# Laying each activation block of a seven-product block multiplication at an offset of its own within 64 bytes

## The chip, the cores and the metric

The kernel runs on one core of one Trainium2 chip. The metric is the time on the device in microseconds (us); the median of three runs stands for a kernel. Of every kernel there is also one profiled execution, whose span and instructions the tables below give.

## What is computed

One layer of a decoder over 528 positions (16 learned meta tokens and 512 tokens) of width 2048, all in float32: an input projection, eight heads of stick-breaking attention beside a gated short convolution, an output projection with residual, and a SwiGLU feed-forward part with residual. Only the feed-forward part, and the arrays that it works on, is touched here:

```python
n2 = _rmsnorm(h, g_ffn[l])                                     # 528 x 2048
h = h + (jax.nn.silu(n2 @ w_gate[l]) * (n2 @ w_up[l])) @ w_down[l]   # w_gate, w_up 2048 x 5632; w_down 5632 x 2048
return h[:, N_META:]
```

## The kernel before

Everything is transposed: channels lie on the 128 partitions, tokens along the free axis. To keep float32 accuracy with TensorE's faster fp32r operands, each operand is cut into a rounded part and a rest (`shi`, `slo` for weights; parts 0 and 1 of an activation block), and a product is three matmuls: rounded by rounded, rounded weight by rest, rest by rounded. Each takes 128x128 weights, and every MATMUL comes with an LDWEIGHTS of its own.

The feed-forward part takes a two by two block product with seven multiplications (Strassen's, in Winograd's form) in place of eight. The weights of a *pair* (gate and up rows of one of 44 groups of 128 hidden channels, or two groups of output channels) are four quadrants, and ACT and DVE form sums of them (`add_quads`, L564 and L584) and cut them in two (`split_quad`, L557 and L558). The activations are cut into four blocks (two halves of the tokens, two halves of the channels), from which seven activation blocks are made once, each `[128, 2, 8, 256]`: two parts, eight channel groups, 256 tokens. They stay in SBUF for the whole stage. These are the tiles `f0` to `f6` (`f_tile`, `fpool` and `fpool_last`). Two of the 44 groups are done beforehand as plain fp32 products; the other 42 go through `pair_product`, which calls `block_product` seven times, with blocks 0 to 6 in order. A `block_product` is, for each of eight channel groups k, the three matmuls of L609 to L611 with 256 moving columns from the activation block: 24 matmuls.

`gate` forms silu(gate) times up, the blocks of the next product, and `store_acts` cuts them and writes them to DRAM (`fd`, L772, on POOL's queue). The down projection walks over four chunks of the hidden dimension (6, 6, 5 and 5 groups deep); `load_acts` reads the seven blocks of a chunk back into a ring of twelve tiles `r0` to `r11` (L825, two DMAs a block, on POOL's queue), the first seven slots (`ring_a`) over the memory of `f0` to `f5`, the last five (`ring_b`) behind them, from the end of `f5` on. Each chunk has eight `pair_product`s whose `block_product`s are six or five groups deep: 18 or 15 matmuls. The ring also gives one tile, `hh`, for the residual in the last chunk.

The number of matmuls of L609 to L611 follows: 42 x 7 x 24 = 7056 on `f` tiles and 8 x 7 x 3 x (6 + 6 + 5 + 5) = 3696 on `r` tiles, 10752 in all, each with 256 columns.

The places of the tiles: a partition of SBUF is one row of bytes. Before, every `f` and `r` tile starts at a multiple of 64 bytes, and all tiles in one place mod 256; the weight tiles `shi` and `slo` start 32 bytes past a multiple of 64. Within a tile the step from group to group is 1024 bytes for activations and 512 for weights. The tile framework tracks every tile by its bytes: a tile that is laid where another one was waits for that one's last reader. In the stage before, operands stand otherwise: the weights `whi`, `wlo` of the projections at multiples of 64; the `nh`, `nl` tiles (normalised input) 32 past a multiple of 64, of which the products `pk` and `pv` take columns in two halves of 264 (the first at 32 past, the second at a multiple of 64), the convolution's products `pc` and `pu` two halves of 258 (at 16 and at 24 past), and `pq` and `pb` 512 columns at 32 past; the output projection `po` takes 512 columns at a multiple of 64 from `oah`, `oal`, `och`, `ocl`.

The order of instructions on each engine is that of the program; the split of the weights runs three block products ahead (`S_AHEAD`).

Of the kernel before, what the change touches and what calls it, by code (L numbers as in the profile page):

```python
# [15 lines left out]
P = 128  # L16
# [9 lines left out]
T2 = SEQ // 2  # L26
# [7 lines left out]
def hybrid_layer(ctx: ExitStack, tc: tile.TileContext, xT, w_in, w_out, w_gu, w_down, vecs, out):  # L34
# [12 lines left out]
    def open_pool(name, bufs=1, **kw):  # L47
        return tc.alloc_tile_pool(name=name, bufs=bufs, reuse_waits="tile", **kw)
# [166 lines left out]
    ms, r, eps_r2, r2 = accs[1], rpool.tile([P, L], F32, name="r"), accs[1], acc  # L215
# [486 lines left out]
    r_h = [acc_h[:, None, t * T2 : (t + 1) * T2].to_broadcast([P, 4, T2]) for t in range(2)]  # L702
    n_f = [0]

    def f_tile(dt, i):

        n_f[0] += 1
        pool = fpool if i < 6 else fpool_last
        return pool.tile([P, 2, 8, T2], dt, tag=f"f{i}", name=f"f{i}_{n_f[0]}")


    (a11, a21), (a12, a22) = ((b[:, 0], b[:, 1]) for b in blocks)
    acts = [None] * 7
    acts[:4] = [f_tile(F32R, i) for i in range(4)]
    w, v, u = (f_tile(F32, i) for i in (4, 5, 6))

    def halves_of_k(op, *blks):
# [12 lines left out]
    def split_act(i, src):  # L730
        if acts[i] is None:
            acts[i] = f_tile(F32R, i)
        halves_of_k(lambda h, l, s: split(h, l, s), acts[i][:, 0], acts[i][:, 1], src)
# [77 lines left out]
    rings_p = [open_pool("ring_a")]  # L811
    rings, n_ring = {}, [0]

    def ring_tile(dt, name):
        i = n_ring[0] % 12
        n_ring[0] += 1
        return rings_p[i // 7].tile([P, 2, 6, T2], dt, tag=f"r{i}", name=name)

    def load_acts(c, s):
        if c < len(CHUNKS):  # L820
            n = CHUNKS[c]
            rings[c, s] = ring_tile(F32R, f"r{c}_{s}")[:, :, :n]

            for part in range(2):
                gp.dma_start(rings[c, s][:, part], fd[c][s][:, part], max_dma_last_dim=3072)  # L825
# [6 lines left out]
    for c in range(len(CHUNKS)):  # L832
        end = c == len(CHUNKS) - 1
        if end:
            hh = ring_tile(F32, "hh")
        for j in range(KT // 2):

            if 1 <= j <= 5:
                load_acts(c + 1, j - 1)
            c1 = cpool.tile([P, 2, T2], F32, tag="c1", name=f"d1_{c}_{j}")  # L840
            c2 = cpool.tile([P, 2, T2], F32, tag="c2", name=f"d2_{c}_{j}")
            if end:
                h2 = [hh[:, :, 2 * (j % 3) + m] for m in range(2)]
                for m in (1, 0):
                    gp.dma_start(h2[m], two(hs[2 * j + m]))
            x = pair_product([rings[c, s] for s in range(7)], c1, c2)
            if j == KT // 2 - 1:
                for s in (5, 6):
                    load_acts(c + 1, s)
            if end:  # L850
                ve.tensor_tensor(c2, c2, h2[1], ALU.add)
                nc.sync.dma_start(two(out[2 * j + 1]), c2)
                ve.tensor_tensor(c1[:, 0], c1[:, 0], h2[0][:, 0], ALU.add)
                ve.tensor_tensor(c1[:, 1], x, h2[0][:, 1], ALU.add)
                nc.sync.dma_start(two(out[2 * j]), c1)
            else:
                sc.copy(c1[:, 1], x)
                gp.dma_start(two(hs[2 * j + 1]), c2, accum_op=ALU.add)
                gp.dma_start(two(hs[2 * j]), c1, accum_op=ALU.add)
# [59 lines left out]
```

## Time and profile before

| | |
|---|---|
| median of 3 runs | 2166.58 us (2165.41 to 2168.12) |
| profiled execution | 2165.52 us, span 2163.8 us |
| granted TensorE clock, mean | 0.995 |
| TensorE matmuls busy | 2136.8 us (99%) |
| weight loads busy | 2026.1 us (94%) |
| VectorE busy | 1551.9 us (72%) |
| ScalarE busy | 997.6 us (46%) |
| GpSimd busy | 378.7 us (18%) |
| mean DMA rate | 149 GB/s |

The span is the stretch from first to last instruction; the time of the execution has 1.7 us more. In the profile, PE is the matmuls and PEld the weight loads; a matmul's listed duration contains its passage through the array, so that successive matmuls overlap, and what one of them costs in a row of many is the distance from its start to the next one's start, called its pitch here. Idle time is put down to the instruction or DMA whose end came last.

### The profile page before, as it was taken

How to read it: one execution, taken by the hardware profiler on the slowest of the kernel's cores; microseconds unless marked ns; L12 is line 12 of the kernel's file. 1: busy time of each engine (PE TensorE's matmuls, PEld its weight loads, DVE VectorE, ACT ScalarE, POOL GpSimd, SP SyncE). 2: the span in 40 equal slices, each digit the busy share in tenths (PEclk: the TensorE clock that was granted, in tenths of full speed). 3: DMA queues.
4: the chain of work that ended last, by engine and by line, in shares of the span. 5: the costliest groups of instructions: out<-in, count | busy, mean ns of one | idle time of the engine just before them, and what ended most of it. 6: DMA issues, size and time to landing. Idle time of an engine off the chain costs nothing.

```text
span 2163.8 us, 39088 instructions
## 1 busy us (share of the span) xinstructions
PE 2136.8 (99%) x15878; PEld 2026.1 (94%) x15878; DVE 1551.9 (72%) x2021; ACT 997.6 (46%) x1550; POOL 378.7 (18%) x503
## 2 busy tenths in 40 slices
PE   8999999999999999999999999999999899999999
PEld 7999999999988874999999999999999899999999
DVE  8777777433353337888888888888888677777787
ACT  5666565322233323544444444445444344444444
POOL 4111111101015440111110110110111222112110
PEclk9999999999999999999999999999999999999999
DMA  5221222222234422454554554544554997869774
GB/s 169 78 79 69 78 79 79 90 96 98 88 128 151 141 102 88 150 162 151 151 164 144 159 152 140 164 151 142 166 151 145 322 298 199 256 158 292 174 214 141
DMA packets 135764, 322.53 MB, mean 149 GB/s; under 512 B 12432, under 2 KB 52368, under 8 KB 135584
## 3 DMA queue, kind: packets, MB, share of 16 engines
q1 hardware_dynamic: 67680, 214.07, 29.8%
q0 software_dynamic: 67904, 105.96, 18.6%
q8 instruction: 124, 2.03, 0.4%
q14 instruction: 56, 0.46, 0.1%
HBM read 258.64 MB, written 61.34 MB: 148 GB/s over the span
## 4 chain that ended last, share of the span: by engine, by line
PE 54%; DMA 3%; DVE 1%; issue 0%; ACT 0%; POOL 0%; DVEq 0%; POOLq 0%; ACTq 0%
PE x L609 10%; PE x L610 10%; PE x L611 10%; PE z L611 5%; PE z L609 5%; PE z L610 5%; PE y L611 3%; PE y L610 3%; PE y L609 3%; DMA b<-w_down 1%; DMA r<-fd 1%; DVE slo L558 0%; ACT shi L557 0%; POOL fd L772 0%; DVE t L564 0%
## 5 line engine op out<-in xcount | busy, mean ns | idle before, releaser
L557 ACT CAST shi<-t 128x1024 fp32r<-128x1024 f32 (+2 forms) x296 | 277.0, 936 | 398.1 <-PE y L610 111.1
L558 DVE TENSOR_TENSOR slo<-t,shi 128x1024 fp32r<-128x1024 f32 (+2 forms) x296 | 319.9, 1081 | 127.9 <-ACT shi L557 126.9
L609 PE MATMUL x<-f,shi 128*128 128x256 f32 x1344 | 379.1, 282 | 1.4 <-ACT u L630 0.7
L610 PE MATMUL x<-f,shi 128*128 128x256 f32 x1344 | 378.2, 281 | 0.0
L611 PE MATMUL x<-f,slo 128*128 128x256 f32 x1344 | 378.2, 281 | 0.0
L137 DVE TENSOR_TENSOR wlo<-raw,whi 128x512 fp32r<-128x512 f32 (+1 forms) x258 | 187.8, 729 | 207.3 <-ACT whi L136 206.6
L557 ACT CAST shi<-b 128x1024 fp32r<-128x1024 f32 (+2 forms) x222 | 207.9, 936 | 271.9 <-PE x L610 165.8
L136 ACT CAST whi<-raw 128x512 fp32r<-128x512 f32 (+1 forms) x258 | 158.1, 614 | 266.1 <-PE po L170 70.6
L609 PEld LDWEIGHTS x<-f,shi 128*128 128x128 f32 x1344 | 253.8, 189 | 2.4 <-ACT p L626 1.0
L610 PEld LDWEIGHTS x<-f,shi 128*128 128x128 f32 x1344 | 253.9, 189 | 0.2 <-issue 0.2
L611 PEld LDWEIGHTS x<-f,slo 128*128 128x128 f32 x1344 | 253.9, 189 | 0.0
L558 DVE TENSOR_TENSOR slo<-b,shi 128x1024 fp32r<-128x1024 f32 (+2 forms) x222 | 239.2, 1077 | 18.5 <-ACT shi L557 14.4
L772 POOL DMA_DIRECT2D fd<-s x154 | 108.5, 915 | 782.1 <-DVE s L183 748.8
L609 PE MATMUL x<-r,shi 128*128 128x256 f32 x704 | 199.6, 284 | 7.7 <-DVE d L634 4.6
L610 PE MATMUL x<-r,shi 128*128 128x256 f32 x704 | 199.4, 283 | 1.5 <-DMA r<-fd 1.5
L611 PE MATMUL x<-r,slo 128*128 128x256 f32 x704 | 199.4, 283 | 0.5 <-DVE slo L558 0.5
L609 PE MATMUL z<-f,shi 128*128 128x256 f32 x672 | 189.3, 282 | 1.7 <-ACT p L628 1.7
L610 PE MATMUL z<-f,shi 128*128 128x256 f32 x672 | 189.1, 281 | 0.0
L611 PE MATMUL z<-f,slo 128*128 128x256 f32 x672 | 189.1, 281 | 0.0
L564 DVE TENSOR_TENSOR t<-b,b 128x1024 f32<-128x1024 f32 (+2 forms) x148 | 159.8, 1080 | 19.2 <-DMA b<-w_down 15.5
L609 PEld LDWEIGHTS x<-r,shi 128*128 128x128 f32 x704 | 134.1, 191 | 8.8 <-issue 4.8
L610 PEld LDWEIGHTS x<-r,shi 128*128 128x128 f32 x704 | 133.9, 190 | 2.0 <-DMA r<-fd 2.0
(310 smaller groups left out, 5421.0 us busy)
## 6 DMA issues: line engine op xcount, KB each, us to landing
b<-w_gu SPq DMA_DIRECT2D x168, 512.0 KB, 3.3
raw<-w_in SPq DMA_DIRECT2D x92, 512.0 KB, 3.2
fd<-s POOLq DMA_DIRECT2D x154, 256.0 KB, 4.0
b<-w_down SPq DMA_DIRECT2D x64, 384.0 KB, 5.0
r<-fd POOLq DMA_DIRECT2D x28, 768.0 KB, 13.3
b<-w_down SPq DMA_DIRECT2D x64, 320.0 KB, 3.7
r<-fd POOLq DMA_DIRECT2D x28, 640.0 KB, 11.7
raw<-w_out SPq DMA_DIRECT2D x32, 512.0 KB, 3.3
```

The source lines that it names most:

```text
L136: sc.copy(hi[:, :c], raw)
L137: ve.tensor_tensor(lo[:, :c], raw, hi[:, :c].bitcast(F32), ALU.subtract)
L557: sc.copy(hi, src)
L558: ve.tensor_tensor(lo, src, hi.bitcast(F32), ALU.subtract)
L564: ve.tensor_tensor(sums[name], a, b, ALU.add)
L609: pe.matmul(ps, hi[:, kk], act[:, 0, k], start=start and k == 0, stop=False, skip_group_check=not start)
L610: pe.matmul(ps, hi[:, kk], act[:, 1, k], start=False, stop=False, skip_group_check=not start)
L611: pe.matmul(ps, lo[:, kk], act[:, 0, k], start=False, stop=k == n - 1, skip_group_check=not start)
L772: gp.dma_start(fd[c][s][:, :, k], t[:, :, i])
```

## The change

Each activation tile gets 16 float32 elements (64 bytes) more per partition, and the block is laid inside at an offset of its own: 2, 4, 6, 10, 12, 14 and 16 elements in `f0` to `f6`, and 1, 2, 3, 5, 7, 9, 11, 13, 14, 15, 8 and 4 in `r0` to `r11`. In bytes past a multiple of 64 the `f` blocks start at 8, 16, 24, 40, 48, 56 and 0, the `r` blocks at 4, 8, 12, 20, 28, 36, 44, 52, 56, 60, 32 and 16. The weight tiles stay where they are. No instruction is added or taken away on any engine. The tiles are longer by 64 bytes, so later ones move up, and some of them now touch a neighbour's old place.

```diff
+    def shifted(pool, dt, n, off, tag, name):
+
+        t = pool.tile([P, 2 * n * T2 + 16], dt, tag=tag, name=name)
+        return t[:, off : off + 2 * n * T2].rearrange("p (a k t) -> p a k t", a=2, k=n)
+
     def f_tile(dt, i):
 
         n_f[0] += 1
         pool = fpool if i < 6 else fpool_last
-        return pool.tile([P, 2, 8, T2], dt, tag=f"f{i}", name=f"f{i}_{n_f[0]}")
+        return shifted(pool, dt, 8, (2, 4, 6, 10, 12, 14, 16)[i], f"f{i}", f"f{i}_{n_f[0]}")
...
     def ring_tile(dt, name):
         i = n_ring[0] % 12
         n_ring[0] += 1
-        return rings_p[i // 7].tile([P, 2, 6, T2], dt, tag=f"r{i}", name=name)
+        return shifted(rings_p[i // 7], dt, 6, (1, 2, 3, 5, 7, 9, 11, 13, 14, 15, 8, 4)[i], f"r{i}", name)
```

## The prediction

> **What bounds the kernel now.** I read the busy rows of the page first, then the chain that ended last, then the stages by windows, then PE's waits in the feed-forward part.
>
> ```profile
> PE 2136.8 (99%) x15878; PEld 2026.1 (94%) x15878; DVE 1551.9 (72%) x2021; ACT 997.6 (46%) x1550; POOL 378.7 (18%) x503
> ...
> PE x L609 10%; PE x L610 10%; PE x L611 10%; PE z L611 5%; PE z L609 5%; PE z L610 5%; PE y L611 3%; PE y L610 3%; PE y L609 3%; DMA b<-w_down 1%; DMA r<-fd 1%; DVE slo L558 0%; ACT shi L557 0%; POOL fd L772 0%; DVE t L564 0%
> ```
>
> The chain runs through the block products' own matmuls for 54% of the span, and hardly through anything else in that part. So the time there is a count of matmuls times a pitch (start to start), and the windows give the pitch (columns: stretch, its length, busy us with the count for each engine, granted clock, DMA share, GB/s):
>
> ```profile
> 471.10:482.30 11.20, 11.20 (x96) 11.20 (x95) 3.37 (x5) 2.36 (x4) 0.00 (x0) 1.00 0.25 85
> 482.60:493.40 10.80, 10.80 (x48) 8.71 (x47) 4.88 (x7) 3.05 (x5) 0.00 (x0) 1.00 0.26 91
> 686.20:696.90 10.70, 10.70 (x48) 8.81 (x47) 4.23 (x6) 3.56 (x6) 5.34 (x5) 1.00 0.40 138
> 1000.00:1600.00 600.00, 600.00 (x5071) 599.86 (x5070) 503.45 (x544) 290.89 (x391) 74.76 (x106) 1.00 0.51 154
> 1740.00:1940.00 200.00, 199.34 (x1685) 199.17 (x1684) 153.75 (x189) 92.80 (x147) 38.83 (x48) 1.00 0.82 227
> ```
>
> 600 us hold 5071 block-product matmuls on `f` tiles: 118.3 ns each. The second stretch on `r` tiles gives 199.34/1685, also 118.3 ns. The granted clock is 1.00 in both. The first three lines are a product `pu` (258 columns), a `pb` (512, start 32 past a multiple of 64) and a `po` (512, start on a multiple); I use them below. The waits of PE from 850 us on are few:
>
> ```profile
> PE x L609 <- DVE d L634: 4.6, 3, 2.6
> PE x L609 <- ACT p L626: 2.9, 2, 2.3
> PE z L609 <- ACT p L628: 1.7, 1, 1.7
> PE x L610 <- DMA r<-fd: 1.5, 2, 0.8
> ```
>
> These are at the handover to the down projection and at the starts of its chunks; a wait named for a DVE or ACT instruction long done there is mostly the `r` load.
>
> **The change part by part: the pitch.** 10752 matmuls, 7056 on `f` and 3696 on `r`, get a new moving start; at 118.3 ns they are 1272 us, so 1% of pitch is 12.7 us. No row shows a block product at another offset, so I bound the price by the rows of other products, taken from start to start in the timeline, first to last of one product. `pu`: 471.01 to 482.36 us, 95 steps, 119.45 ns. `pv`, 264 columns, half of them at 32 past: 252.06 to 258.52, 53 steps, 121.9 ns. `po`: 686.17 to 696.93, 47 steps, 228.96 ns. `pb`: 482.48 to 493.45, 47 steps, 233.5 ns.
>
> Moving starts on a multiple of 64 are those of the block products and `po`. From them a column costs (228.96 - 118.33)/256 = 0.432 ns. By that law 258 columns should take 119.20 ns, 264 should take 121.8, and 512 should take 228.96. The shifted rows stand above it by 0.25 ns (258), by about 0.1 (264) and by 4.55 (512, which is 2.3 ns if it goes by columns and is halved for 256). Inside `pu` the starts alternate, hardly scattered: from a half that starts 16 past to the next start it is 118.0 ns, from one that starts 24 past it is 120.9. Against 119.2 that is -1.2 and +1.7 ns. Either the place mod 16 counts, or the two halves only trade time and their mean is what a start costs; the row can't tell.
>
> So the lower end is -1.2 ns for every shifted matmul and the upper one +2.3 ns. I sort by place mod 16. Offsets of 4, 12 and 16 elements (`f1`, `f4`, `f6`, 1008 matmuls each) stay on a multiple of 16 bytes, as do 8 and 4 in the ring (`r10`, `r11`). Following the ring's counter, these two hold two blocks of a chunk six deep and two of a chunk five deep, 2 x 144 + 2 x 120 = 528 matmuls. The rest, 4 x 1008 = 4032 and 3696 - 528 = 3168, together 7200, start off a multiple of 16. For them I take half of the +1.7, 0.85 ns, since the mean over the two halves says that part of it is traded; for the 3552 others zero. 7200 x 0.85 = 6.1 us, all on the path, as PE has no gaps there. 2496 of the ring's matmuls start at an odd multiple of 4 bytes, of which no row has an example; I price them like the others and let the range carry the doubt.
>
> **DVE and ACT on shifted tiles.** The seven blocks are made from 820 to 877 us by DVE and ACT, with DVE near the path. Rows of the same engines on shifted and on aligned operands (medians in the middle):
>
> ```profile
> L490 ACT ACTIVATE tmp<-tmp,vec x8: 724/724/726, 378.1 to 620.0; 128x512 f32<-128x512 f32 x8
> L492 DVE SCALAR_TENSOR_TENSOR tmp<-tmp,vec,tmp x16: 747/752/753, 379.2 to 621.9; 128x512 f32<-128x512 f32 x16
> L507 ACT ACTIVATE och<-tmp,vec x8: 724/726/726, 393.9 to 632.9; 128x512 fp32r<-128x512 f32 x8
> L508 DVE SCALAR_TENSOR_TENSOR ocl<-tmp,vec,och x8: 750/751/753, 394.7 to 633.7; 128x512 fp32r<-128x512 f32 x8
> ```
>
> L490 reads from 8 bytes past, L492 from 12 and 16 past; the aligned ones cost the same within 2 ns. Zero.
>
> **New waits from the longer tiles.** Three, each with its cover. (1) The topmost block buffer now reaches both `hb` buffers, so the first scaling on DVE (L722, at 820.2 us) also waits for the last stores of `hb`; the last is issued at 811.6 and these land within 4.1 us, by 815.7. Cover 4.5 us. (2) `r3` now reaches 64 bytes into `f3`, so its load waits, on POOL's queue, for the fourth instead of the third block product of the last pair; behind it in the queue stand `r4` to `r6` and the `fd` and `hd` stores. The last matmul on `f3` starts at 1694.5 us. The loads are issued so:
>
> ```profile
> 1692.19 5.87 POOL L825 DMA_DIRECT2D r<-fd  x8
> 1698.30 0.70 POOL L825 DMA_DIRECT2D r<-fd  x1 [0.24 <-issue]
> ```
>
> Eight in 5.87 us, 0.73 each: `r3`'s two are the seventh and eighth, from 1696.6 us on. Cover 2 us; without it the load would come late by what is missing, and PE waits for these loads. (3) `r7` now waits for `f6`, whose last matmul is at 1703.1; its load is issued in the first chunk's second pair, after 1720 us. All three: zero.
>
> **The DMA into shifted tiles.** The loads of `r` are on the chain from 1692.9 to 1720.3 us, 27 us without a break worth naming, and PE idles 6.2 us from 1700 to 1730. Their packets of 3072 bytes land at a start not on a multiple of 32 bytes in most slots. No row shows such a landing with rows this long. Upper bound: the only odd rows, `vec` with 300 bytes, are a tiny DMA that landed in 4.2 us; taken by bytes it is far slower, but nothing here is like it. I take 0.3 us, 1% of 27 us: near nothing, since no byte more is moved, with the rival below for the other end.
>
> The sum: 6.1 + 0.3 = 6.4 us. The profiled execution, 2165.52 us, becomes 2171.9; the median stands 1.06 us above it, so 2173.0 us, own range of this case 2169 to 2179.
>
> **The rivals.** *Faster: the one common place was a bad one.* Before, every block stands the same way to the weights that are loaded meanwhile (PEld 599.86 of 600 us busy), so if the two reads meet badly they do so in all 10752 matmuls; the change spreads them. For it: the half of `pu` that starts 16 past is 1.2 ns below the law. At that price 9744 matmuls (all but `f6`, whose place mod 64 is the old one) save 11.7 us: 2154.9 us. It decides if the pitch of the block products holds a stall that depends on the distance of the two reads. Against: `po`, with weights and activations at the same place mod 64, and `f`, 32 apart, fit one law with 258 and 264. The Trainium skill (TensorE: Matmul & The Clock Gate, Part 2) says that PE reads moving operand and weights through two independent ports, so that loading the next weights takes nothing from the running matmul; by that rule this rival has no ground and the sum would lack any gain. No run here shows the ports apart. I give it 0.26.
>
> *Each ragged start costs a whole piece.* If the moving row is read in pieces of 16 bytes, 256 columns are 64 pieces on a multiple of 16 and 65 off it; a piece is 4 columns, 1.73 ns, and 7200 of them 12.4 us: 2179 us. By pieces `pu` would have to take 120.06 ns, by columns 119.20; it takes 119.45, nearer to the columns, which speaks against. At `pb`'s price, 2.3 ns for all 9744, it is 22.4 us: 2189 us. The Trainium skill (SBUF — State Buffer, Specifications) has SBUF in lines of 16 bytes, and each crossing to a new line pays a penalty; by that rule the change costs, and the trace agrees in part only, by the 0.25 ns of `pu`. I give it 0.17.
>
> *Nothing.* The halves of `pu` trade time, and starts don't count: 2166.6 us. For it: `pv`'s 0.1 ns. 0.12.
>
> *The loads become late.* If packets into ragged rows took a quarter longer, the 27 us of loads would grow by 7 us and the later chunk starts by 1 each: 10 us, 2177 us. 0.05.
>
> **How the numbers follow.** The forecast has 0.40. A change under 0.2%, 4.3 us, about what a measurement of this kernel can tell from none, takes 0.10 of the forecast (its lower part), 0.02 of the faster case and 0.10 of the nothing case: same 0.22. Faster: 0.24 of the first rival and 0.01 of nothing: 0.25. Slower: 0.30 + 0.01 + 0.17 + 0.05 = 0.53. The range takes in the first rival with a little more, 2152, and `pb`'s price with some late loads, 2194.
>
> **What would show it.** A stretch of 600 us in the `f` stage holds about 5050 matmuls instead of 5071 if the forecast is right, 5115 with the faster rival. Taken tile by tile, `f0`, `f2`, `f3` and `f5` (2, 6, 10, 14 elements) must be dearer than `f1` and `f4`, and `f6` must be as before. L182, L183 and L722 must keep their durations, the first L825 issues their times, and the idle time of PE from 1700 to 1730 its 6 us. The prediction is wrong if offsets off a multiple of 16 cost nothing, if odd multiples of 4 cost several ns, or if all shifted blocks get cheaper.

## The result

| | before | after |
|---|---|---|
| median | 2166.35 us (4 runs, 2165.41 to 2168.12) | 2177.73 us (4 runs, 2176.30 to 2178.93) |
| profiled execution's span | 2163.8 us | 2177.2 us |
| ratio | | 1.0051, 95% interval 1.0034 to 1.0069 |

The change costs 11.4 us, 0.5%, clear of the 0.2% that can be told from nothing. The forecast was 2173.0 us, range 2152 to 2194, with slower at 0.53.

### The profile page after: what moved, and what is told of

Same layout as the page of the kernel before. It is cut to its first block, busy times and chain, and to the rows that moved or that the text cites. A ratio compares the mean times of both kernels' runs of the same rounds, so it can differ in the third digit from the quotient of the medians.

```text
span 2177.2 us, 39090 instructions
## 1 busy us (share of the span) xinstructions
PE 2147.8 (99%) x15878; PEld 2037.2 (94%) x15878; DVE 1550.8 (71%) x2021; ACT 997.1 (46%) x1550; POOL 379.4 (17%) x503
## 4 chain that ended last, share of the span: by engine, by line
PE 56%; DMA 2%; DVE 0%; issue 0%; ACT 0%; POOL 0%; ACTq 0%; DVEq 0%; POOLq 0%
PE x L609 11%; PE x L611 11%; PE x L610 11%; PE z L609 5%; PE z L611 5%; PE z L610 5%; PE y L611 3%; PE y L609 3%; PE y L610 3%; DMA r<-fd 1%; DMA hd<-d 0%; DMA b<-w_down 0%; ACT shi L557 0%; DVE slo L558 0%; POOL fd L777 0%
## 5 line engine op out<-in xcount | busy, mean ns | idle before, releaser
L557 ACT CAST shi<-t 128x1024 fp32r<-128x1024 f32 (+2 forms) x296 | 276.3, 934 | 407.4 <-PE y L610 118.4
L609 PE MATMUL x<-f,shi 128*128 128x256 f32 x1344 | 380.0, 283 | 1.3 <-ACT u L630 0.8
L609 PEld LDWEIGHTS x<-f,shi 128*128 128x128 f32 x1344 | 254.5, 189 | 2.3 <-ACT u L630 1.0
L558 DVE TENSOR_TENSOR slo<-b,shi 128x1024 fp32r<-128x1024 f32 (+2 forms) x222 | 239.0, 1077 | 19.1 <-ACT shi L557 17.4
L609 PE MATMUL x<-r,shi 128*128 128x256 f32 x704 | 200.5, 285 | 8.9 <-DVE d L634 4.2
L609 PE MATMUL z<-f,shi 128*128 128x256 f32 x672 | 190.0, 283 | 1.7 <-ACT p L628 1.7
L609 PEld LDWEIGHTS x<-r,shi 128*128 128x128 f32 x704 | 134.9, 192 | 10.4 <-issue 4.8
```

The source lines that it names most:

```text
L557: sc.copy(hi, src)
L558: ve.tensor_tensor(lo, src, hi.bitcast(F32), ALU.subtract)
L609: pe.matmul(ps, hi[:, kk], act[:, 0, k], start=start and k == 0, stop=False, skip_group_check=not start)
```

## The profile after

The busy rows and the chain of the page of after:

```profile
PE 2147.8 (99%) x15878; PEld 2037.2 (94%) x15878; DVE 1550.8 (71%) x2021; ACT 997.1 (46%) x1550; POOL 379.4 (17%) x503
...
PE x L609 11%; PE x L611 11%; PE x L610 11%; PE z L609 5%; PE z L611 5%; PE z L610 5%; PE y L611 3%; PE y L609 3%; PE y L610 3%; DMA r<-fd 1%; DMA hd<-d 0%; DMA b<-w_down 0%; ACT shi L557 0%; DVE slo L558 0%; POOL fd L777 0%
```

PE and its weight loads grew, by 11.0 and 11.1 us with the same 15878 matmuls; DVE, ACT and POOL kept their busy time within 1.1 us. The same two stretches of the block products by windows of after (length, busy us with counts by engine, clock, DMA share, GB/s):

```profile
1000.00:1600.00 600.00, 600.00 (x5027) 600.00 (x5026) 498.12 (x539) 288.54 (x389) 72.25 (x104) 1.00 0.50 151
1740.00:1940.00 200.00, 199.21 (x1667) 199.03 (x1667) 152.32 (x185) 91.38 (x146) 41.08 (x51) 1.00 0.82 228
```

5027 matmuls in place of 5071: the mean pitch is 119.4 ns instead of 118.3, at the same granted clock 1.00 (the prediction's signs were 5050 for its forecast, 5115 for the faster rival). So there are fewer matmuls in the same time, not a slower clock and not a wait. One pair of the `f` stage of after, cut at the first matmul of each block, shows where (the first two columns are the stretch and its length; each holds 24 starts, and the counts include those still in passage):

```profile
1147.28:1150.20 2.92, 2.92 (x27) 2.92 (x26) 2.50 (x3) 1.33 (x2) 0.00 (x0) 1.00 0.37 130
1150.20:1153.04 2.84, 2.84 (x27) 2.84 (x25) 2.84 (x5) 1.32 (x2) 0.00 (x0) 1.00 0.13 51
1153.04:1155.92 2.88, 2.88 (x27) 2.88 (x26) 2.33 (x4) 2.48 (x3) 0.00 (x0) 1.00 0.52 182
1155.92:1158.81 2.89, 2.89 (x27) 2.89 (x25) 2.89 (x3) 1.32 (x2) 1.61 (x3) 1.00 0.17 42
1158.81:1161.61 2.80, 2.80 (x26) 2.80 (x25) 2.25 (x4) 1.05 (x1) 1.93 (x3) 1.00 1.10 246
1161.61:1164.49 2.88, 2.88 (x26) 2.88 (x25) 2.40 (x3) 1.05 (x1) 0.00 (x0) 1.00 1.21 336
1164.49:1167.34 2.85, 2.85 (x26) 2.85 (x25) 2.08 (x3) 1.37 (x2) 0.00 (x0) 1.00 0.67 213
```

Before, each of these blocks takes 2.84 us. Now `f0`, `f2`, `f3`, `f5` (8, 24, 40, 56 bytes) take 2.88 to 2.92, `f1` 2.84, `f4` (48 bytes) 2.80, `f6` 2.85. DVE, ACT and DMA work differ freely between the lines, and the lengths do not follow them.

The waits of PE from 850 us on, and the issue of the ring's loads, of after (its L830 is L825 of before):

```profile
PE x L609 <- DVE d L634: 4.2, 2, 3.1
PE x L609 <- ACT p L626: 2.8, 2, 2.2
PE x L610 <- DMA r<-fd: 2.6, 2, 2.0
PE z L609 <- ACT p L628: 1.7, 1, 1.7
...
```

```profile
1697.76 6.59 POOL L830 DMA_DIRECT2D r<-fd  x9
```

The loads go out 0.73 us apart with no gap where `r3` waits for `f3`, as before. PE's idle time in the 30 us around the handover is 7.8 us (1705 to 1735), against 6.2 from 1700 to 1730 before.

The span's 13.4 us divide so, by the first and last block-product matmul of the two traces: the `f` stage starts 1.5 us earlier (861.4 against 862.9) and is 7.2 us longer (847.5 against 840.3), the down projection is 7.6 us longer (464.4 against 456.8). Pitch by tile, from the starts of successive matmuls of one block in the trace, without steps over 200 ns: 119.43 ns on `f` and 119.70 on `r`, against 118.38 and 118.47. That is 1.05 x 7056 = 7.4 us and 1.23 x 3696 = 4.5 us; the remaining 3 us of the down projection are waits: the long steps exceed a pitch by 22.2 us in all, against 19.1.

## The experiments

Pitches are means by tile, taken as just said. *Place* is where the moving row starts; *distance* is that minus the start of the weight row, mod 256. In the kernel before, every block has the place 192 mod 256 and the weights 224, so the distance is 224. Each matmul has its own weight load, which runs beside the matmul ahead of it. Pitches come from the one profiled execution of a kernel. The edits are shown shortened; a line in words stands for the lines of code that set these places.

### The layout without the offsets

```diff
-        return shifted(pool, dt, 8, (2, 4, 6, 10, 12, 14, 16)[i], ...)
+        return shifted(pool, dt, 8, 16, ...)        # r tiles likewise
```

> The tiles are 64 bytes longer as in the change, with its new waits, but every block starts 64 bytes in, on a multiple of 64 as before. If the start's place within 64 bytes makes the difference (both the theory of the place and that of the distance to the weights), every tile's pitch is 118.3 ns and the time that of before, 2166 us within 3. If the tiles' spread over 256 bytes or the new waits cost part of it, the pitch differs from tile to tile (f6 of the changed kernel, which starts on a multiple of 64, stands at 118.9) or PE idles more, and the time is 2169 to 2178 us.

The stretch from 1000 to 1600 us:

```profile
1000.00:1600.00 600.00, 600.00 (x5067) 600.00 (x5067) 501.91 (x544) 290.59 (x391) 74.05 (x105) 1.00 0.51 154
```

Measured: 2166.38 us, ratio 1.0005 (0.9996 to 1.0015). The longer tiles and their new waits cost nothing that can be told; the offsets make the difference. The time is that of before, but the pitch is not that of before in every tile: each tile is 64 bytes longer, so successive tiles stand 64 bytes further on mod 256, and `f` at 0, 64, 128 and 192 has 116.9, 120.0, 118.7 and 118.2 ns. Good and bad places happen to average out, at 118.5.

### Other offsets

```diff
+  f: offsets (1, 3, 5, 7, 9, 11, 13), 256 bytes more per tile
+  r: offsets (2, 4, 6, 8, 10, 12, 14, 2, 4, 6, 8, 10), 128 bytes more per tile
```

> Other offsets: f0 to f6 start 4, 12, 20, 28, 36, 44 and 52 bytes past a multiple of 64 (1, 3, 5, 7, 9, 11, 13 elements) with the tiles kept in one place mod 256, the ring at 8, 16, 24, 32, 40, 48, 56, 8, 16, 24, 32, 40. Theory of the place mod 16 (read from the changed kernel's r tiles, where 4, 20, 36, 52 stand at 120.2 to 121.5 ns and 12, 28, 44, 60 at 117.6 to 119.4): f0, f2, f4, f6 near 120.8 ns, f1, f3, f5 near 118.5, r at 8, 24, 40, 56 near 120.3 and at 16, 32, 48 near 118. Theory of an element off a multiple of 8 bytes: all f tiles alike, near 120. Theory that only the stage counts (r differs from f by its depth): no order by the place mod 16 in f. Total by the first theory about 2181 us.

Measured: 2181.15 us (one run). `f` at 4, 20, 36, 52: 120.7, 122.2, 123.2, 122.0 ns. At 12, 28, 44: 118.0, 118.1, 117.8. `r` at 8, 24, 40, 56: 120.7 to 121.0; at 16, 32, 48: 117.2, 120.0, 117.2. So against before 4 mod 16 costs 3.7 ns here, 8 mod 16 somewhat over 2, and 12 mod 16 nothing. In the changed kernel's `r` the first costs 2.3 and the last 0.2. The sizes are not pure, since the distance changes with the place; the order holds in `f` as in `r`. "Off a multiple of 8" and "only the stage" fall. Multiples of 16 are not all alike.

### Place or distance: all blocks at 8, with and without the weights

```diff
+  every offset 2 elements (all_8)
+  the same, and shi and slo laid 2 elements into tiles 64 bytes longer (all_8_weights_8)
+  the kernel before, only shi and slo 2 elements into tiles 256 bytes longer (weights_8)
```

> Every block starts 8 bytes past a multiple of 64 (2 elements); weights where they are. Place theory (8 mod 16 costs about 2 ns): pitch 120.3 ns on all tiles, 10752 x 2.0 = 21 us more, 2187 us. Distance theory (8 minus 32 is -24, at which f0 of the changed kernel had 121.1 ns): 121.1 ns, 30 us more, 2196 us. Theory that it is the mixture of offsets from block to block that costs: 118.3 ns, 2167 us.

> As the one before, and the split weights moved by 8 bytes too (40 past a multiple of 64), so that the distance of the two reads is that of before. Distance theory: 118.3 ns, 2167 us. Place theory: the moving start alone counts, as without the move of the weights, 2187 us, plus what ragged weights cost, if anything (a weight row of 512 bytes off a multiple of 16 would be one 16-byte piece more in 32).

> The activations as in the kernel before, the split weights alone moved by 8 bytes (40 past a multiple of 64). Theory that the moving row's place alone counts: 118.3 ns, 2166 us. Theory of the distance: the -8 bytes between them are off a multiple of 16 as in all_8, near 120.3 ns, 2187 us. Theory that ragged weights cost by themselves (all_8_weights_8 stood 0.3 ns above all_8 in the f stage): 118.6 ns, 2169 us.

The stretch from 1000 to 1600 us of each, in that order (one run each):

```profile
1000.00:1600.00 600.00, 600.00 (x4996) 600.00 (x4995) 495.55 (x536) 286.37 (x386) 71.04 (x101) 1.00 0.50 151
```

```profile
1000.00:1600.00 600.00, 600.00 (x4987) 600.00 (x4986) 494.72 (x534) 285.12 (x385) 71.61 (x102) 1.00 0.50 151
```

```profile
1000.00:1600.00 600.00, 600.00 (x5037) 600.00 (x5036) 499.86 (x541) 289.38 (x390) 73.81 (x105) 1.00 0.52 152
```

All at 8: 120.2 ns on `f`, 120.3 on `r`, 2184.85 us; the mixture of offsets within 64 bytes is not the cause. Moving the weights along does not give it back: 120.5 and 120.7 ns, 2182.72 us, where the distance theory said 118.3. The distance is that of before only mod 64 there: the weight tiles too are 64 bytes longer, so each block meets the distances 32, 96, 160 and 224. But pad_only has the same four and 118.5 ns on average, so the conclusion stands. Moving only the weights by 8 costs less than half: 119.2 and 119.3 ns, 2170.18 us, where the distance theory said 120.3. So for a start off a multiple of 16 it is the moving row's own place that counts, 1.7 to 1.9 ns at 8 mod 16 (against pad_only and before). Weights alone at 8 mod 16 cost some 0.9 ns, three times what was expected; whether by their own place or by the distance, now 216, no run separates. The two do not add up.

### Undoing the ragged part alone

```diff
-  f: (2, 4, 6, 10, 12, 14, 16)   r: (1, 2, 3, 5, 7, 9, 11, 13, 14, 15, 8, 4)
+  f: (0, 4, 4, 8, 12, 12, 16)    r: (0, 0, 0, 4, 4, 8, 8, 12, 12, 12, 8, 4)
```

> The changed kernel with every offset rounded down to a multiple of 4 elements (f: 0, 4, 4, 8, 12, 12, 16; r: 0, 0, 0, 4, 4, 8, 8, 12, 12, 12, 8, 4), so that blocks still stand at different places within 64 and 256 bytes, but each starts on a multiple of 16. Theory that the starts off a multiple of 16 cost the time: pitch 117 to 120 ns by tile, 118.3 on average, 2166 us within 4. Theory that the spread of places as such costs it: 119.5 ns on average, 2177 us.

The stretch from 1000 to 1600 us:

```profile
1000.00:1600.00 600.00, 600.00 (x5127) 600.00 (x5126) 507.63 (x550) 294.39 (x398) 74.05 (x105) 1.00 0.52 155
```

Measured: 2159.45 us, ratio 0.9972 (0.9961 to 0.9983): not only back, but below the kernel before. Rounding the offsets down takes 0.8% off the changed kernel, 17 to 18 us. Tile by tile, `f0`, `f2`, `f3`, `f5` go from 121.1, 119.8, 120.7, 119.9 ns to 118.2, 115.5, 113.6, 118.2, while `f1`, `f4`, `f6`, which did not move, stay within 0.4. Not all of the 17 to 18 us is the price of ragged starts. Rounding also moves the distances, of `f2` to 112 and of `f3` to 192, and these two end 2.9 and 4.8 ns below before, which on 1008 matmuls each is 7.8 us. What the ragged starts cost against the kernel before is the 12.4 us worked out below. The blocks of this kernel that stand out, by windows cut as above (`f2` and `f3`):

```profile
1147.34:1150.10 2.76, 2.76 (x26) 2.76 (x25) 2.29 (x4) 2.48 (x3) 0.00 (x0) 1.00 0.49 190
1150.10:1152.83 2.73, 2.73 (x26) 2.73 (x25) 2.73 (x3) 1.32 (x2) 1.33 (x3) 1.00 0.03 9
```

### Multiples of 16: place or distance mod 256

```diff
+  the kernel before, 64 bytes ahead of f0 and of r0 (base_0)
+  the same, and shi and slo 64 bytes into tiles 256 bytes longer (base_0_weights_64)
```

> The kernel before with 64 bytes ahead of f0 and of r0 and nothing else, so that every block starts on a multiple of 256 bytes instead of 192 past one; weights where they are. In pad_only the f tiles at 0 mod 256 had 116.9 ns, those at 64 120.0, at 128 118.7 and at 192 118.2. Theory that the place mod 256 counts on its own, tile by tile: 116.9 ns on all tiles, 10752 x 1.4 = 15 us less than before, 2151 us. Theory that these differences only exist between neighbours of different place: 118.3 ns, 2166 us.

> As base_0, and the split weights moved by 64 bytes as well, so that the distance to the moving rows is that of before in every bit. Theory of the distance to the weights (for starts on a multiple of 16): 118.3 ns, 2166 us. Theory of the place of the moving row alone: as base_0, 116.9 ns, 2151 us.

The same stretch of base_0, then of base_0_weights_64:

```profile
1000.00:1600.00 600.00, 600.00 (x5145) 600.00 (x5145) 508.88 (x551) 295.79 (x400) 75.56 (x107) 1.00 0.54 156
```

```profile
1000.00:1600.00 600.00, 600.00 (x5073) 600.00 (x5072) 502.60 (x544) 291.39 (x392) 74.17 (x105) 1.00 0.53 154
```

base_0 (distance 32): 116.7 and 117.3 ns, 2151.78 us, ratio 0.9938 (0.9923 to 0.9952). A lead of 64 bytes, and no other edit, makes the kernel 0.6% faster than before. With the weights moved along, the distance is again 224 and the pitch that of before to a hundredth on `f`: 118.38 (118.52 on `r`, 118.47 before), 2162.97 us (one run). Here the distance counts and the place does not.

### All distances in steps of 16

```diff
+  f: distances 0, 16, 64, 80, 128, 192, 240; r: 48, 176, 96, 160, 112, 224, 144, 240, 128, 208, 32, 192
```

> All sixteen distances (moving start minus weight start, mod 256) in steps of 16 bytes, tile by tile: f0 to f6 at 0, 16, 64, 80, 128, 192, 240, the ring at the other nine and three again. Theory that the distance counts for starts on a multiple of 16: 32 again 116.7 to 117.3 as in base_0, 96 near 120.0, 160 near 118.7, 224 near 118.2 as in pad_only, and the same value where f and r have the same distance. Theory that a tile's place in memory or in the sequence of blocks counts: no agreement with those numbers. A distance below 116.7 would make a kernel faster than base_0. Total near 2166 us.

Measured: 2163.77 us (one run). 96 has 119.9 ns, 160 118.4, 224 118.2, as foreseen; 112 has 115.7, 192 has 114.4 on `f` and 114.7 on `r`; 0 and 128 are dear (119.7 to 120.1). But 32 has 117.8 where base_0 had 117.3 on `r`, 16 has 118.9 where rounded_16 had 116.7 on `f`, 80 has 119.5 where rounded_16 had 118.2, and 240 has 117.0 on `f` and 118.3 on `r`. There is agreement at most distances, not at all. The mean is 118.2 ns over the seven distances of `f` and 118.3 over the twelve of `r`, so the distance of before, with 118.4, is an average one.

### The distance that looked best

```diff
+  the kernel before, 224 bytes ahead of f0 and of r0 (base_160)
+  the kernel before, shi and slo 32 bytes into tiles 256 bytes longer (weights_32)
```

> The kernel before with 224 bytes ahead of f0 and of r0, so that every block starts at 160 mod 256, which is 192 past the weights; nothing else. In rounded_16 and survey_16 the tiles at this distance had 113.6 to 114.7 ns. Theory of the distance mod 256: 114 ns on all tiles, 10752 x 4.3 = 46 us less than before, 2120 us, as long as DVE and ACT (DVE 84% busy in the f stage) keep up with weights that are wanted 4% sooner. Theory that such tiles only gain between neighbours at other distances: 118.3 ns, 2166 us.

> The activations as in the kernel before (192 mod 256); the split weights alone moved by 32 bytes, to 0 mod 256, so that the distance is 192 as in base_160, reached from the other side. Theory of the distance: 114 ns, 2120 us. Theory of the moving row's place alone: 118.3 ns, 2166 us.

Both stand at distance 192 throughout. base_160: 2154.81 us, ratio 0.994 (0.9923 to 0.9958); weights_32: 2147.38 us (one run), the lowest time of all. Both are faster than before, but by 12 and 19 us instead of 46:

```profile
1000.00:1600.00 600.00, 600.00 (x5097) 600.00 (x5096) 504.63 (x547) 293.07 (x395) 74.23 (x105) 1.00 0.52 154
```

```profile
1000.00:1600.00 600.00, 600.00 (x5097) 600.00 (x5096) 504.69 (x546) 292.25 (x394) 74.06 (x105) 1.00 0.51 154
```

The same 5097 matmuls in the same 600 us confirm that in the `f` stage the distance decides, from whichever side it is reached. But the pitch on `f` is 117.45 ns, not 114. The steps of the `f` stage have two patterns: 541 of base_160's are 113 or 114 ns, nearly all others 117 to 119, and a block in the second pattern takes 2.83 us, again and again, without any wait. In rounded_16 the tile at this distance comes after one at another distance and runs at 113 and 114. So the same distance has at least two steady patterns.

The two traces also show when the pattern changes. In both, the 20 blocks from about 899 us on are in the fast pattern. One late start ends it, a step of 174 ns at 954.01 us in base_160 (at 953.53 in weights_32), and the slow pattern then holds for all the blocks up to the handover. These are base_160's lines around it:

```profile
953.79 0.28 PE L610 MATMUL x<-f,shi 128*128 128x256 f32 x1
953.90 0.28 PE L611 MATMUL x<-f,slo 128*128 128x256 f32 x1
954.01 0.34 PE L609 MATMUL z<-f,shi 128*128 128x256 f32 x1
954.19 0.28 PE L610 MATMUL z<-f,shi 128*128 128x256 f32 x1
954.30 0.28 PE L611 MATMUL z<-f,slo 128*128 128x256 f32 x1
```

In the down projection, too, every change of pattern between blocks stands beside a step of more than 150 ns, though not every such step brings one. There 109 of base_160's 224 blocks are in the fast pattern and 169 of those of weights_32, which is why their pitches on `r` differ, 115.95 and 114.78 ns, at one distance. So the delay that went before chooses the pattern. That was seen, not tested; how to keep the faster one stays open.

### Ragged start or ragged end

```diff
+  f offsets (2, 0, 6, 0, 10, 0, 14); L610 and L611 with 254 of 256 columns
```

> The second and third matmul of each triple (L610 and L611 of the kernel before) take 254 of the 256 columns: the rests of the last two tokens of each half are left out. f0, f2, f4 and f6 start 8 past a multiple of 16 and end on one; f1, f3 and f5 start on one and end 8 past. Steps between the two short matmuls, by columns 0.86 ns below those of 256. Theory that a ragged start costs: 119.5 ns in f0, f2, f4, f6 and 117.4 in f1, f3, f5. Theory that a ragged end costs: the other way round, 117.4 and 119.5. Theory that each costs a piece: all alike, near 119.5. No total is forecast from it.

Measured: 2270.33 us (one run), with 62.3 us of waits of PE at L609 for the copy of L626 and a mean clock of 0.981, which was not foreseen and is not explained. Between the two short matmuls, again without steps over 200 ns: 117.7, 115.0 and 118.0 ns in `f1`, `f3`, `f5`, where the start is even and the end ragged; 120.3, 121.0, 117.8 and 119.7 in `f0`, `f2`, `f4`, `f6`, where it is the other way round (`f2` stands behind the waits). That leans to the start. But `f4` speaks against it, and the three tiles of the first group differ by 3 ns at one and the same distance, so it is not settled.

## Why the prediction was right, and where its steps were off

**The bound.** PE's pitch times 10752 was the right quantity: of the 13.4 us of span 12 are pitch.

**The price of the pitch** was the term that was mis-sized. The prediction took 0.85 ns, half of the +1.7 ns of `pu`'s ragged halves, for 7200 matmuls. Measured against before: 2.00 ns on the 4032 of `f`, 1.37 on the 3168 of `r`, 1.72 on average; 8.1 + 4.3 = 12.4 us. The thought that the two halves merely traded time was the step that failed. The dearer half of `pu` starts at 8 mod 16, and at that place the unhalved row was the price: 2.0 ns on `f`, and 1.8 more than before in all_8, where no half can trade with another. That 1.7 also fits the average over all 7200 is luck: 2496 of them start at odd multiples of 4, and there 1.3 ns is a mean of 2.3 and 0.2. The forecast of 6.4 us was thus somewhat over half of the 11.4 measured.

**The sorting by place mod 16** held for `f`, and tile by tile as was said (`f0`, `f2`, `f3`, `f5` dearer, `f1` as before). It failed in two points: "the others at zero" hides `f4`, which gained 1.3 ns, and `f6`, which lost 0.6; and the odd multiples of 4, priced alike, split into 4 mod 16, which is dearest, and 12 mod 16, which is free. One of the prediction's own signs of being wrong, several ns at odd multiples of 4, thus came half true.

**No cost on DVE and ACT; the three covers.** L727 of after, which is L722 of before, has its median at 1218 ns against 1220; the loads' issues keep their spacing, and pad_only the time of before. Right.

**The DMA into ragged rows.** 3 us more of waits in the down projection, where 0.3 was put. Such waits vary: 22.1 us in rounded_16 and 23.7 in base_160, without ragged rows, 16 in all_8_weights_8 with them. So the ragged rows are not shown to be the cause, and nothing supports the rival of late loads.

**The faster rival** was right in its ground and wrong in its outcome. The distance of the two reads does set the pitch: base_0 shows a gain of 0.6%. But the common distance was an average one, so that spreading the blocks brings nothing on average (118.5 ns in pad_only, 118.2 and 118.3 over the distances of survey_16); only choosing does. The argument that `po` and `f` fit one law was empty, since that law is the line through these two points. The Trainium skill (TensorE: Matmul & The Clock Gate, Part 2) says that moving operand and weights come through two independent ports, so that a weight load takes no read bandwidth from the running matmul. The prediction read this as leaving no ground for the rival. Here base_0 and base_0_weights_64, 116.7 and 118.4 ns on `f`, differ only in where the split weights lie: whatever the ports do, the place of the weights counts, and the measurement decides.

**The rival of a whole piece** gave 2179 us, nearest to the measurement, by a law that is not what was found. The Trainium skill (SBUF — State Buffer, Specifications) puts the lines at 16 bytes; the trace agrees that 16 is the grain, but one more line would cost alike at 4, 8 and 12 mod 16, and in survey_f4 and all_8 they cost 3.7, 1.8 and nothing.

## What to carry to other kernels

Where PE has no gaps, the bytes at which operands start belong to the tuning: keep the moving rows on multiples of 16 bytes, and try the distance between moving and weight rows mod 256 by a lead of some multiple of 16 bytes, which adds no instruction. Measure the pitch tile by tile: one kernel with a different offset in each tile is a survey, and its total, a mean over good and bad places, tells little. When a row of the profile has a ragged half that is dearer, take its price whole before explaining it away, and bound it from both sides.

## What the runs showed of the hardware that was not expected

The pitch of a 128x128 fp32r matmul with 256 columns, as a mean over a tile, lay between 113.6 ns (`f3` of rounded_16) and 123.2 (`f4` of survey_f4) at a granted clock of 1.00, with the same matmuls and only the starts of the operands changed. Where all blocks have one distance and start on a multiple of 16, the same distance gives the same pitch in the `f` stage whichever operand is moved (118.38 in before and in base_0_weights_64; 117.45 and 117.44 in base_160 and weights_32). Where the tiles differ in distance, it need not (16: 118.9 and 116.7). At one distance two steady patterns, near 113.3 and 117.8 ns, were seen in the same kernel, and they changed over only beside a late start; one step of 174 ns left the slower one standing for over 6000 matmuls. Why the distance counts, why a late start changes the pattern, and why 12 mod 16 is free, is not explained by any run here.
